# A two-layer transformer step: sums of weight chunks issued one chunk ahead, contraction halves in turn, and the norm's row spread over three chunks

## The chip, the cores and the metric

The kernel runs on one core of a Trainium2 chip. The metric is the device time of one execution in microseconds (us). The profile calls the engines PE (TensorE matmul), PEld (TensorE weight load), DVE (VectorE), ACT (ScalarE), POOL (GpSimd) and SP (SyncE, which issues most DMAs). Each engine works through its own list of instructions in the order in which the program issues them.

## What is computed

256 tokens of width 1024 pass through two layers. In each, a first feed-forward, a mixer and a second feed-forward are added to the residual; a norm ends it. All is float32.

```python
def swiglu(x, w_gate, w_up, w_down):          # 1024 -> 2816 -> 1024
    return (silu(x @ w_gate) * (x @ w_up)) @ w_down

for layer in range(2):
    x = x + 0.5 * swiglu(rms_norm(x), ...)     # feed-forward 1 (3)
    h = rms_norm(x)
    x = x + (hybrid mixer if layer == 0 else short convolution mixer)(h)
    x = x + 0.5 * swiglu(rms_norm(x), ...)     # feed-forward 2 (4)
return rms_norm(x, final_norm)
```

The hybrid mixer is a gated MLP over token chunks next to causal attention of four heads; the convolution mixer is `(b * conv3(c * xin)) @ w_out` with three projections b, c, xin.

## The kernel before

**Weights and parts.** Every float32 product is made from two parts of each operand: a high part, rounded to the matmul's format, and a low part, the remainder. `Weights` streams the weights in chunks of 1 MB. A chunk is loaded into one of five raw buffers (`load_piece`, L71, a DMA of SyncE's queue), its high part is made on ScalarE (`high`, L93) and its low part on VectorE (`low`, L98). The low part frees the raw buffer, and that lets the next load be issued. `W.next()` hands out the parts of a chunk and first calls `catch_up` (L108): high parts up to three chunks ahead (`AHEAD`), low parts up to two ahead, then whatever was queued with `afterwards` (L105).

**Sum units.** A feed-forward has 22 blocks of 128 columns: two in the opening pair of chunks (`open_pairs`), three plain units of four blocks each (`plain`, four chunks), and two sum units (`summed`, seven products each). A sum unit computes a 2 by 2 block product with seven products in place of eight; the operands are sums and differences of blocks. The sums of weights are VectorE instructions over whole chunks (`sum`, L90): one for product 1, two for product 2 and one for product 6 of the unit. In `catch_up` (L111) they are issued directly ahead of the high part of their chunk. The sums of activations are made by `Sums.make` (L490), each with a high part on ScalarE and a low part on VectorE (L503).

**The order of a feed-forward** is written out by hand: `ORDER = "nnsnsnsnssnsnsnsnsnssnsssn"`, where n is the next chunk of a plain unit and s the next product of a sum unit. Letters counted from 0 are called steps. A plain step has 24 matmuls of 512 columns, a sum step 12 (`mm_n`, L293 to L295). After each step the loop of L622 calls `run_later()`, which takes one entry of a list and may turn a finished block with four transposes into PSUM bank `misc(1)` (`turned`, L523), and then what `head` (L621) holds for that step. The turned block is read from the bank by `split`: a high part on ScalarE (L402) and a low part on VectorE (L405). The last sum unit's two turns are called those of r, the plain units' those of v.

**The norm.** The rows are scaled by the inverse root only after the first matmuls. `column` (L366) has two matmuls for the sum of squares (L369) and a chain of ten small VectorE operations (`rsqrt`, L306 to L317). `broadcast` (L373) makes two diagonal tiles on VectorE (L377), a matmul that spreads them over the partitions (L379) and a copy on ScalarE (L381). In `ffn`, `column` stands ahead of the two `added` calls (a ScalarE copy, L415, and a VectorE add, L421, which read the opening pairs from PSUM); `first`, with `broadcast`, the gating of the opening pair and `xs.gained`, follows step 0.

**After the steps.** The down projection of the first three feed-forwards takes `mm_run` (L274: two matmuls of 512 columns, two of 256, for two blocks), with a `run_later()` ahead of each half. The fourth keeps tokens on partitions (L1078 on); there `back` (L1045) first turns the residual back with 16 transposes and four VectorE copies (L1055). In the hybrid mixer two projections for the gate use `t_pair` with `mm_run`; `gate` (L901) adds the two halves of the PSUM tile and multiplies by the row. In the convolution mixer `column` stands after the first two projections and `broadcast` after the third (L1011 to L1021). In the first feed-forward, hook 20 runs `turn_small` (L716), whose transposes use `misc(1)` too.

The lines that set the order of the sums before:

```python
    def catch_up(self):
        n = min(len(self.items), self.used + AHEAD)
        while self.highs < n:
            self.sum(self.highs)
            self.high(self.highs, 0, self.tile(self.highs).shape[1])
        self.flush(min(len(self.items), self.used + AHEAD - 1))
```

## Time and profile before

| | |
|---|---|
| three runs | 1002.9, 1004.84, 1005.6 us; median 1004.84 |
| the profiled execution | 1002.79 us, of which the span of instructions is 1000.9 us |
| TensorE (PE) busy | 940.8 us, 94%, 4884 matmuls |
| weight loads (PEld) | 798.1 us, 80%, beside the matmuls |
| VectorE (DVE) busy | 729.7 us, 73% |
| ScalarE (ACT) busy | 505.0 us, 50% |
| mean granted TensorE clock | 0.981 |

A busy PE is modelled from its instructions' starts and lasts past the start of the next, so 94% is no measure of its rate; the idle time before a matmul, and what ended it, tells where TensorE stood still. In a timeline, the number in brackets is the idle time before the first instruction of the row, and behind the arrow stands what ended it.

### The profile page before, as it was taken

What the parts mean: (1) busy time and instruction counts of PE and PEld (TensorE: products, weight loads), DVE (VectorE), ACT (ScalarE), POOL (GpSimd) and SP (SyncE); (2) the same over time, 40 slices, a digit from 0 to 9 for tenths busy, and PEclk for the clock granted to TensorE, in tenths of its full rate; (3) what the DMA queues carried; (4) which work ended last, traced back from release to release, by engine and by line L of the source; (5) the groups of instructions that cost most, each with busy time, mean ns of one, the idle gap of its engine ahead of it and who ended that gap; (6) DMA issues with size and microseconds to landing.
All of it is one profiled execution on the core that took longest, in us unless ns stands there. A gap on an engine that the chain in (4) does not pass through costs nothing.

```text
span 1000.9 us, 11781 instructions
## 1 busy us (share of the span) xinstructions
PE 940.8 (94%) x4884; PEld 798.1 (80%) x4884; DVE 729.7 (73%) x742; ACT 505.0 (50%) x512; POOL 2.8 (0%) x9
## 2 busy tenths in 40 slices
PE   7989889999899989999999999999899988999897
PEld 6778778888788778778877887788899877877786
DVE  6799876566567899884758989664667768889552
ACT  6555554444645665453436556443444544656342
POOL 0000000000000000000000000000000000000000
PEclk9899999999999999999999999999999999999999
DMA  9257565647144355685424565847554515747601
GB/s 330 93 169 230 168 211 179 207 162 233 61 151 145 103 175 196 212 259 187 165 96 160 171 210 181 278 145 238 168 169 152 185 46 167 267 132 271 210 22 43
DMA packets 121169, 173.82 MB, mean 174 GB/s; under 512 B 3408, under 2 KB 69532, under 8 KB 121116
## 3 DMA queue, kind: packets, MB, share of 16 engines
q1 hardware_dynamic: 120780, 172.53, 52.3%
q8 instruction: 38, 0.62, 0.3%
q10 hardware_dynamic: 336, 0.54, 0.1%
q14 instruction: 15, 0.12, 0.0%
HBM read 172.01 MB, written 1.05 MB: 173 GB/s over the span
## 4 chain that ended last, share of the span: by engine, by line
PE 72%; DVE 16%; ACT 5%; issue 3%; DMA 3%; SPq 0%; DVEq 0%; ACTq 0%
PE ps L279 15%; PE ps L294 9%; PE ps L295 9%; PE ps L293 9%; PE ps L281 7%; DVE wlo L98 7%; PE ps L271 4%; DVE raw L90 3%; PE misc L294 3%; PE misc L295 2%; PE misc L293 2%; PE ps L287 2%; PE ps L289 2%; PE ps L288 2%; PE ps L272 2%
## 5 line engine op out<-in xcount | busy, mean ns | idle before, releaser
L93 ACT ACTIVATE whi<-raw 128x2048 fp32r<-128x2048 f32 (+2 forms) x196 | 354.7, 1824 | 216.3 <-DVE raw L90 97.7
L98 DVE TENSOR_TENSOR wlo<-raw,whi 128x2048 fp32r<-128x2048 f32 (+2 forms) x196 | 423.7, 2179 | 24.6 <-ACT whi L93 24.3
L294 PE MATMUL ps<-wlo,x 128*128 128x512 f32 x512 | 205.2, 401 | 16.1 <-DVE wlo L98 16.1
L293 PE MATMUL ps<-whi,x 128*128 128x512 f32 x512 | 207.9, 406 | 5.9 <-DVE ev_u L421 3.2
L295 PE MATMUL ps<-whi,x 128*128 128x512 f32 x512 | 204.4, 399 | 0.0
L279 PE MATMUL ps<-hx,whi 128*128 128x512 f32 x528 | 166.9, 397 | 0.0
L294 PEld LDWEIGHTS ps<-wlo,x 128*128 128x128 f32 x512 | 99.5, 194 | 40.0 <-DVE wlo L98 19.6
L293 PEld LDWEIGHTS ps<-whi,x 128*128 128x128 f32 x512 | 99.3, 194 | 26.9 <-DVE ev_u L421 3.3
L281 PEld LDWEIGHTS ps<-hx,wlo 128*128 128x128 f32 x528 | 99.0, 187 | 24.1
L295 PEld LDWEIGHTS ps<-whi,x 128*128 128x128 f32 x512 | 99.0, 193 | 21.4
L281 PE MATMUL ps<-hx,wlo 128*128 128x256 f32 x528 | 105.4, 281 | 0.0
L387 DVE SCALAR_TENSOR_TENSOR xT<-ps,xT 128x512 f32<-128x512 f32 x40 | 27.5, 691 | 74.4 <-PE ps L281 67.6
L279 PEld LDWEIGHTS ps<-hx,whi 128*128 128x128 f32 x528 | 80.8, 189 | 0.0
L90 DVE TENSOR_TENSOR raw<-raw 128x2048 f32<-128x2048 f32 x32 | 73.2, 2287 | 3.3 <-DMA raw<-in_ffn_w_up 3.0
L287 PE MATMUL ps<-x,whi 128*128 128x256 f32 x192 | 54.6, 284 | 0.0
L288 PE MATMUL ps<-x,whi 128*128 128x256 f32 x192 | 54.3, 283 | 0.0
L289 PE MATMUL ps<-x,wlo 128*128 128x256 f32 x192 | 54.3, 283 | 0.0
L271 PE MATMUL ps<-x,whi 128*128 128x512 f32 x128 | 45.2, 395 | 0.5 <-ACT whi L93 0.5
L405 DVE TENSOR_TENSOR hx<-misc,hx 128x512 fp32r<-128x512 f32 x40 | 27.5, 687 | 23.2 <-ACT hx L402 23.2
L402 ACT ACTIVATE hx<-misc 128x512 fp32r<-128x512 f32 x40 | 23.6, 589 | 27.9 <-PE misc L530 27.9
L288 PEld LDWEIGHTS ps<-x,whi 128*128 128x128 f32 x192 | 36.8, 192 | 0.0
L287 PEld LDWEIGHTS ps<-x,whi 128*128 128x128 f32 x192 | 36.8, 192 | 0.0
(247 smaller groups left out, 1179.2 us busy)
## 6 DMA issues: line engine op xcount, KB each, us to landing
raw<-in_ffn_w_gate SPq DMA_DIRECT2D x43, 1024.0 KB, 5.3
raw<-in_ffn_w_up SPq DMA_DIRECT2D x43, 1024.0 KB, 5.1
raw<-in_ffn_w_down SPq DMA_DIRECT2D x34, 1024.0 KB, 5.2
raw<-in_conv_w_in SPq DMA_DIRECT2D x12, 1024.0 KB, 5.3
raw<-in_hyb_w_in SPq DMA_DIRECT2D x10, 1024.0 KB, 6.1
raw<-in_ffn_w_down SPq DMA_DIRECT2D x12, 768.0 KB, 4.8
raw<-in_hyb_w_out SPq DMA_DIRECT2D x4, 1024.0 KB, 5.3
raw<-in_conv_w_out SPq DMA_DIRECT2D x4, 1024.0 KB, 5.1
```

The lines of the kernel that those rows point to most:

```text
L90: self.nc.vector.tensor_tensor(self.raw[dst][0], self.raw[x][0], self.raw[y][0], op=op)
L93: self.nc.scalar.activation(self.part(i, "whi")[:, s:e], self.tile(i)[:, s:e], AF.Copy)
L98: self.nc.vector.tensor_tensor(lo[:, s:e], raw[:, s:e], hi[:, s:e].bitcast(F32), op=ALU.subtract)
L271: nc.tensor.matmul(dst, whi, x, start=start, stop=False, skip_group_check=True)
L279: nc.tensor.matmul(dst, ws[i][0], xs[i], start=start and i == 0, stop=False, skip_group_check=True)
L281: nc.tensor.matmul(dst[:, :S], ws[i][1], xs[i][:, :S], start=False, stop=stop and i == n - 1, skip_group_check=True)
L287: nc.tensor.matmul(dst[:, :S], whi, x[:, :S], start=start, stop=False, skip_group_check=True)
L288: nc.tensor.matmul(dst[:, :S], whi, x[:, S:], start=False, stop=False, skip_group_check=True)
L289: nc.tensor.matmul(dst[:, :S], wlo, x[:, :S], start=False, stop=stop, skip_group_check=True)
L293: nc.tensor.matmul(dst, xhi, whi, start=start, stop=False, skip_group_check=True)
L294: nc.tensor.matmul(dst, xhi, wlo, start=False, stop=False, skip_group_check=True)
L295: nc.tensor.matmul(dst, xlo, whi, start=False, stop=stop, skip_group_check=True)
```

## The change

- The sums of a chunk are no longer issued with its high part. `sums(n)` keeps its own count, and `catch_up` calls it last, for one chunk beyond the high parts; so the sums of a chunk stand on VectorE behind the low part and the queued operations of the step before.
- A plain unit takes its chunks as gate, up, gate, up, each pair one half of the contraction; two PSUM tiles are open side by side, and silu comes after the third chunk, not the second.
- `column` now ends with the two diagonal tiles. In a feed-forward it follows step 0, `first` follows step 1, and `xs.make(0)` step 2. The two `added` calls stand ahead of it all.
- The turns of a sum unit come one step later (`turned(..., 2)`).
- In the hybrid mixer the two gate projections use `mm_s` (three matmuls of 256 columns into one half of PSUM), and `gate` is one multiply from PSUM.
- In the convolution mixer `column` follows the third projection and `broadcast` the fourth.
- `back` moves from ahead of the last down projection into it, behind the third block of weights; the PSUM tiles there are named.

```diff
-    def sum(self, i):
-        for dst, x, y, op in self.items[i].sums:
-            self.nc.vector.tensor_tensor(self.raw[dst][0], self.raw[x][0], self.raw[y][0], op=op)
+    def sums(self, n):
+        while self.summed < min(len(self.items), n):
+            for dst, x, y, op in self.items[self.summed].sums:
+                self.nc.vector.tensor_tensor(self.raw[dst][0], self.raw[x][0], self.raw[y][0], op=op)
+            self.summed += 1
...
         while self.highs < n:
-            self.sum(self.highs)
+            self.sums(self.highs + 1)
             self.high(self.highs, 0, self.tile(self.highs).shape[1])
         self.flush(min(len(self.items), self.used + AHEAD - 1))
+        self.sums(self.used + AHEAD + 1)
...
     def plain_unit(g, u, c):
-        for w in (g, u):
-            for k in range(0, KB, 4):
+        for k in range(0, KB, 4):
+            for w in (g, u):
                 yield chunk(w[:, k:k + 4, c])
...
             rsqrt(self.rstd, m[:, :NT], 1.0 / D)
+            self.diag = act.tile([P, NT, P], F32, tag="diag", bufs=1, name="diag")
+            for t in range(NT):
+                nc.vector.tensor_scalar(self.diag[:, t], ident, self.rstd[:, t:t + 1], None, op0=ALU.mult)
...
-            later.extend([None, lambda: turn(0), None, lambda: turn(1)])
+            later.extend([None] * n + [lambda: turn(0)] + [None] * (2 - n) + [lambda: turn(1)])
...
-            s = []
-            for j in range(2):
-                p = ps(1 + j)
-                for i in range(2):
+            p, s = [None, None], []
+            for i in range(2):
+                for j in range(2):
                     w = W.next()
+                    if i == 0:
+                        p[j] = ps(1 + j)
...
-                        turned(v, f)
+                            times(p[1][:, t], t, v[t], s[t])
+                        turned(v, f, 1)
...
-            turned([q16, q15], f)
+            turned([q16, q15], f, 2)
...
         ps_pairs = opened or open_pairs(norm.x)
-        norm.column()
         g0, u0 = (added(p, tag) for p, tag in zip(ps_pairs, ("ev_g", "ev_u")))
...
-        head = {0: first, 1: lambda: xs.make(0), 3: lambda: xs.make(1), 5: lambda: xs.make(2), 6: lambda: xs.make(3)}
+        head = {0: norm.column, 1: first, 2: lambda: xs.make(0), 3: lambda: xs.make(1), 5: lambda: xs.make(2),
+                6: lambda: xs.make(3)}
...
     def gate(p):
-        u = by_token(added(p, "ev_u"), norm.rbc, "ev_u")
+        u = act.tile([P, 2 * S], F32, tag="ev_u", bufs=2, name="u")
+        nc.vector.tensor_tensor(pair(u), p[:, :, :S], norm.rbc2, op=ALU.mult)
...
-    u_ps = t_pair(norm.x, scores)
+    u_ps = t_pair(norm.x, scores, mm_s)
...
-    u_ps = t_pair(norm.x, mix)
+    u_ps = t_pair(norm.x, mix, mm_s)
...
-    norm.column()
     W.catch_up()
     cp, xp = first[0], pair(first[1])
     bp = pair(copied(conv_pair(), "ev_u"))
+    norm.column()
     W.flush()
+    cn = copied(conv_pair(), "ev_g")
     norm.broadcast()
...
-            cn = copied(conv_pair(), "ev_g")
...
-            p2 = ps()
+            p2 = ps(1 + c)
...
-    back()
...
-    p0, p1 = ps(), ps()
+    p0 = ps(0)
...
             down(y0[t], w, fs[0], fs, t, 0, 512)
+        if fs[0] == 8:
+            back()
+    p1 = ps(1)
```

## Rows read from the trace of the kernel before

**Rows 1.** The page, part 1: busy time and share of the span by engine.

```profile
PE 940.8 (94%) x4884; PEld 798.1 (80%) x4884; DVE 729.7 (73%) x742; ACT 505.0 (50%) x512; POOL 2.8 (0%) x9
```

**Rows 2.** TensorE's waits: line, waited for, total us, times, longest us.

```profile
PE ps L294 <- DVE wlo L98: 16.1, 8, 3.1
```

**Rows 3.** Windows: stretch, length, busy us and instructions by engine, clock, DMA share, GB/s.

```profile
324.00:355.00 31.00, 26.04 (x109) 20.84 (x108) 25.41 (x29) 18.64 (x24) 0.00 (x0) 0.94 0.30 101
329.00:337.00 8.00, 5.53 (x19) 4.12 (x18) 5.62 (x8) 2.33 (x4) 0.00 (x0) 0.79 0.37 131
```

**Rows 4.** Timeline of VectorE, head of the second feed-forward: start us, us, instruction, idle.

```profile
324.64 0.16 DVE L306 TENSOR_SCALAR rs_v<-misc 128x2 f32<-128x2 f32 x1 [4.34 <-PE misc L369]
...
327.69 4.49 DVE L98 TENSOR_TENSOR wlo<-raw,whi 128x2048 fp32r<-128x2048 f32 x2
...
347.12 4.61 DVE L90 TENSOR_TENSOR raw<-raw 128x2048 f32<-128x2048 f32 x2
351.65 2.28 DVE L98 TENSOR_TENSOR wlo<-raw,whi 128x2048 fp32r<-128x2048 f32 x1
...
355.23 0.69 DVE L503 TENSOR_TENSOR xp<-xs,xp 128x512 fp32r<-128x512 f32 x1 [0.70 <-ACT xp L502]
```

**Rows 5.** Timeline of TensorE, head of the second feed-forward.

```profile
328.63 0.39 PE L293 MATMUL ps<-whi,x 128*128 128x512 f32 x1
...
329.77 0.39 PE L295 MATMUL ps<-whi,x 128*128 128x512 f32 x1
332.63 1.22 PE L379 MATMUL misc<-diag,ones 128*128 128x256 f32 x2 [2.47 <-DVE diag L377]
...
353.99 0.50 PE L294 MATMUL ps<-wlo,x 128*128 128x512 f32 x1 [2.49 <-DVE wlo L98]
```

**Rows 6.** The page, part 6: DMA issues, count, KB each, median us to landing.

```profile
raw<-in_ffn_w_up SPq DMA_DIRECT2D x43, 1024.0 KB, 5.1
```

**Rows 7.** Timelines of TensorE and VectorE, heads of feed-forwards 1, 3 and 4.

```profile
55.38 0.50 PE L294 MATMUL ps<-wlo,x 128*128 128x512 f32 x1 [2.91 <-DVE wlo L98]
...
517.98 0.16 DVE L306 TENSOR_SCALAR rs_v<-misc 128x2 f32<-128x2 f32 x1 [5.17 <-PE misc L369]
...
546.27 0.50 PE L294 MATMUL ps<-wlo,x 128*128 128x512 f32 x1 [1.35 <-DVE wlo L98]
...
805.96 0.16 DVE L306 TENSOR_SCALAR rs_v<-misc 128x2 f32<-128x2 f32 x1 [4.34 <-PE misc L369]
...
836.54 0.50 PE L294 MATMUL ps<-wlo,x 128*128 128x512 f32 x1 [2.91 <-DVE wlo L98]
```

**Rows 8.** Timelines of VectorE and TensorE, feed-forward 2, second sum unit and end.

```profile
398.99 0.68 DVE L405 TENSOR_TENSOR hx<-misc,hx 128x512 fp32r<-128x512 f32 x1
...
402.91 4.62 DVE L90 TENSOR_TENSOR raw<-raw 128x2048 f32<-128x2048 f32 x2 [1.03 <-DMA raw<-in_ffn_w_up]
...
409.78 0.50 PE L294 MATMUL ps<-wlo,x 128*128 128x512 f32 x1 [1.14 <-DVE wlo L98]
...
442.94 1.75 DVE L98 TENSOR_TENSOR wlo<-raw,whi 128x1536 fp32r<-128x1536 f32 x1
...
443.08 0.66 PE L530 MATMUL misc<-ident,r 128*128 128x128 f32 x4 [1.67 <-DVE hx L405]
```

**Rows 9.** Timeline of TensorE: turn_small, the convolution mixer, the fourth feed-forward's end.

```profile
130.04 0.33 PE L254 MATMUL misc<-ident,rows 128*128 128x128 f32 x1 [2.30 <-DVE hx L405]
...
719.61 0.70 PE L379 MATMUL misc<-diag,ones 128*128 128x256 f32 x2 [3.18 <-DVE diag L377]
...
926.19 0.55 PE L1052 MATMUL ps<-ident,xT 128*128 128x128 f32 x3 [1.07 <-DVE v L539]
...
934.06 0.63 PE L530 MATMUL misc<-ident,v 128*128 128x128 f32 x4 [2.65 <-DVE hx L405]
```

**Rows 10.** Windows in which mm_run and mm_s run, columns as above.

```profile
455.00:495.00 40.00, 40.00 (x230) 34.80 (x229) 20.83 (x21) 17.25 (x17) 0.00 (x0) 1.00 0.54 178
725.00:765.00 40.00, 40.00 (x335) 40.00 (x335) 28.67 (x37) 17.97 (x17) 0.00 (x0) 1.00 0.53 170
```

More of the change, by code (lines that the diff above doesn't have):

```diff
@@ L58, in __init__ @@
         self.shapes = {name: tuple(src.shape) for name, src in self.src if src is not None}
-        self.loaded = self.highs = self.lows = self.used = 0
+        self.loaded = self.summed = self.highs = self.lows = self.used = 0
         self.raw, self.parts, self.queue = {}, {}, []
@@ L371, in column @@
             rsqrt(self.rstd, m[:, :NT], 1.0 / D)
+            self.diag = act.tile([P, NT, P], F32, tag="diag", bufs=1, name="diag")
+            for t in range(NT):
+                nc.vector.tensor_scalar(self.diag[:, t], ident, self.rstd[:, t:t + 1], None, op0=ALU.mult)
         def broadcast(self):
-            diag = act.tile([P, NT, P], F32, tag="diag", bufs=1, name="diag")
-            for t in range(NT):
-                nc.vector.tensor_scalar(diag[:, t], ident, self.rstd[:, t:t + 1], None, op0=ALU.mult)
             m = misc()
-            nc.tensor.matmul(m[:, :S], ones, diag.rearrange("p t i -> p (t i)"), start=True, stop=True)
+            nc.tensor.matmul(m[:, :S], ones, self.diag.rearrange("p t i -> p (t i)"), start=True, stop=True)
             self.rbc = act.tile([P, 1, S], F32, tag="rbc", bufs=1, name="rbc")
@@ L521, in gated, with turned @@
             h[:2] = split(v, 0, True)
-        def turned(v, f):
+        def turned(v, f, n):
             def turn(q):
@@ L556, in plain @@
                             s.append(act.tile([P, 512], F32, tag="ev_g", bufs=2, name="s"))
-                            silu(s[t], p[:, t], t)
+                            silu(s[t], p[0][:, t], t)
                     if i and j == 1:
@@ L560, in plain @@
                         for t in range(NT):
-                            times(p[:, t], t, v[t], s[t])
-                        turned(v, f)
+                            times(p[1][:, t], t, v[t], s[t])
+                        turned(v, f, 1)
                     yield
```

2 lines of the change are left out of this document (1 added, 1 removed).

## The prediction, made before the change was run

> **What bounds the kernel now.** I read the page first. TensorE is busy for 94% of the span [rows 1], so the only time to win is what it loses between matmuls. The waits of TensorE come next: the largest group is the low part of a weight chunk, 16.1 us in 8 waits [rows 2]. Then I looked at the stretch in which a feed-forward begins, in the windows and the timelines of VectorE and TensorE. There VectorE, not TensorE, sets the pace: 25.41 us busy out of 31 in the second feed-forward, while TensorE has two holes [rows 3 to 5]. The reader should see two things in [rows 4, 5]. The broadcast (L379) waits 2.47 us for diag, which stands behind two low parts of 4.49 us. And the low part of step 5 runs from 351.65, directly behind two sums of 4.61 us, and TensorE stands still for 2.49 us until it is there. I count steps by the letters of ORDER, from 0. A plain step is 24 matmuls, a step of a sum unit 12. From 328.63 to 329.77 five starts took 1.14 us, 0.228 each [rows 5], so these steps take 5.5 and 2.75 us.
>
> **Working.** The profiled execution took 1002.79 us (span 1000.9), 2.05 under the median of 1004.84. The sum is made against 1002.79 and the difference then carried to the median.
>
> *The head of a feed-forward.* Four edits go together here: sums one chunk ahead, column after step 0, diag inside column, first after step 1 and make(0) after step 2. Before, the rsqrt chain of column runs ahead of the two adds that read the opening pairs; it starts at 324.64 [rows 4], having waited for the column matmuls, and the first add could have started about 0.4 earlier, at 324.2, when ScalarE's copy was done. The diag wait goes: in the new order VectorE does adds, two low parts, one sum, rsqrt and diag, about 1.3 + 4.4 + 2.2 + 2.5 = 10.4 us, so diag is there at 334.8, and TensorE wants it after steps 0 and 1, at 324.2 + 11 + 0.4 = 335.6. That hides it by 0.8 us; if that cover is gone, the wait stands again, shorter than 2.47.
>
> What is late next is xs.parts[0], which step 4 multiplies. Its make(0) now follows step 2, and step 2's catch_up puts the two sums of item 6 on VectorE ahead of it. Up to that point the new order asks VectorE for exactly the operations that the old one did before 351.65: rsqrt, two adds, diag, three low parts and the one of step 2, three sums, the gating and xs. Their work is 25.41 less 2.9 for what lies behind 351.65 in the window: 22.5 us [rows 3, 4]. I add 0.7 twice for the round trips through ScalarE (silu, xp), by the 0.70 at 355.23 [rows 4], and 0.4 for hops inside the rsqrt chain, together 24.3. So xs.parts[0] is there at 324.2 + 24.3 = 348.5. TensorE, unhindered through steps 0 to 3, comes to it at 335.9 + 2.75 + 5.5 = 344.2 and waits some 4.4 us: a new stall. Step 4 takes 2.75, step 5 begins at 351.3. Before, its second matmul came at 353.99 [rows 5], as if it had begun at 353.8. The head gains 2.5 us, not the 5 us of its two waits.
>
> Can the two sums start on time? They need a load that the low part of step 1 sets free, at about 337; loads land after 5.1 us [rows 6], at 342.1, just when VectorE is through with what stands before them. I take no wait.
>
> The same sum for the others [rows 7]: in the third, VectorE can begin at 517.98 - 0.4 = 517.6; xs.parts[0] at 541.9, step 5 at 544.7 against 546.27 - 0.2: gain 1.3. In the fourth, 805.96 - 0.4 = 805.6, plus 1.0 because TensorE itself must wait for the adds to free its bank and the broadcast comes later by that; step 5 at 833.6 against 836.3: gain 2.7. In the first, TensorE is late and throttled, VectorE waits about 3 us for the column and for the broadcast, and step 5 comes out at 55.3 against 55.2: 0, with 1.7 either way for the clock.
>
> *The second sum unit.* Before, sums stand between the low part of step 15 and that of step 16, wait 1.03 us for their load, and TensorE then loses 1.14 at step 18 [rows 8]. Ahead of their chunk the sums still need a load freed by the low part just before, plus 5.1. I get sums from 398.9 to 403.4 and the low part at 406.3, with TensorE there at 407.3: that wait goes. But the turn of r is one step later, so its half on VectorE, at 398.99 before and ahead of the sums [rows 8], falls behind them, to 404.1, and the next turn wants the same bank at 402.1: a wait of 2.0. Net, with small change elsewhere, -0.4 in feed-forwards 2 to 4. In the first the small angle operations fill the same place; 0, with the same bounds.
>
> *Step 20 of the first.* turn_small wants the bank that turn has just filled; it waits 2.30 us [rows 9]. The sum of item 24, before in step 21, now stands ahead of the freeing operation: 2.2 us more, a loss.
>
> *The end of a feed-forward.* Before, two turns of r collide and TensorE waits 1.67 us [rows 8]. Now 16 matmuls lie between them (16 times 0.174 [rows 10], 2.8 us), but the next low part (1.75 us, at 442.94 [rows 8]) comes ahead of the freeing operation too: 0.2 + 1.4 + 1.7 + 0.7 = 4.0 us after step 25, against 3.1. 0.8 to 0.9 remain; gain with the overlap 1.1 each in the first three. In the fourth, back moves away from the turns: waits of 1.07 and 2.65 go [rows 9], 1.3 comes: 2.4. Its 16 transposes and four copies are only moved, to a place where both banks are free, so 0; without that cover it costs what it saves.
>
> *Conv mixer.* The wait for diag, 3.18 [rows 9], goes: a whole pair, 48 matmuls at 0.119 [rows 10] or 5.7 us, lies between column and broadcast, against some 5 us of rsqrt, diag and a low part. Convolution starts later against TensorE, but its results are wanted two pairs later. Gain 3.2.
>
> *Hybrid mixer.* mm_s makes three matmuls of 256 columns where mm_run makes 512 + 256. By counts, 40/335 times 3 is 0.358 us, 40/230 times 2 is 0.348 [rows 10]: 32 times 0.010, a loss of 0.3. The Trainium skill, "TensorE: Matmul & The Clock Gate", section "Back-to-back issue gap", gives a warm gap of N/2.4 + 2.5 ns; an estimate by it is 2.5 ns per step more, 0.1 us instead of 0.3, so the row is taken. The gate's copy and add give way to one multiply in the same place of VectorE's queue; 0, bounds -0.7 and +0.7.
>
> *Interleaved halves* (plain): same matmuls, silu one step before times instead of two; a step of 2.75 or more covers it: 0.
>
> *Clock.* A stall can drop the clock to its lower level: 0.79 over 8 us is 1.7 us lost [rows 3]. The 31 us window has 0.94, or 1.9 us, so nearly all of its loss is this one fall, and the wait ending at 353.99 cost none before 355. The new stall at step 4 is longer than either. In feed-forwards 2 and 3 this is a new fall; VectorE, the pacer, takes up part of it: I take 0.7 of 1.7 each, -1.4.
>
> **Sum.** First: 0 + 0 - 2.2 + 1.1 = -1.1. Second: 2.5 - 0.4 + 1.1 = 3.2. Third: 1.3 - 0.4 + 1.1 = 2.0. Fourth: 2.7 - 0.4 + 2.4 = 4.7. Conv 3.2, hybrid -0.3, clock -1.4. Together 10.3: 992.5 for the profiled execution, **994.5** at the median. Bounds of the terms, 1.7 for each head and 2 for each place in the second unit, mostly independent, make 989 to 1000 the forecast's own range.
>
> **Rivals.**
> 1. *The stalls simply go.* If make(0) is not late, the four heads give up to 4.4 each more, 17.6 in all: 977. For it: the change removes every named wait of the heads. Against: 22.5 us of VectorE work must come before step 4 in any order in which the sums of item 6 precede make(0). Chance 0.10.
> 2. *The clock.* Each new stall (step 4, the turn at step 16) costs a full fall. That is 2 more us in the heads and 1.7 in each of three second units, 7 in all: 1001.5. For it: 2.47 us idle was enough for one fall. Against: 2.49 us was not. Chance 0.17.
> 3. *Slower: loads.* Sums ahead in VectorE's one queue wait for a load with every later operation behind them, at items 6 and 19, eight times. Each microsecond by which the load lands later than low part plus 5.1 costs TensorE up to one; from 1.3 us each the gain is used up, at 2.5 us (half a landing) it is 1004.8 + 8 x 1.2 = 1014. For it: one such wait of 1.03 is in the trace already. Against: the median landing is 5.1 us [rows 6], which the sum already holds. Chance 0.08.
> 4. *The sums do not move in effect.* In a busy queue only their place against evictions changes; if heads give nothing and only conv and the last tail remain, less 2.2 and 0.3, the result is about 1002 to 1004. Against: VectorE idles 5.6 of the 31 us of the head [rows 3], and the new order closes most of it. Chance 0.05.
>
> The forecast has 0.60.
>
> **How the numbers follow.** 994.5 is the likeliest case. The range 983 to 1002 takes in that case, the clock, and part of the first rival; outside stay the rest of it, the slower one and part of the fourth. A measurement of this kernel tells about 0.3%, 3 us, from no change, so faster means below 1001.8. That holds for the forecast, the first rival, and most of the second, whose full price ends just on that edge, so that any fall that is missing or partly covered leaves it below: 0.60 + 0.10 + 0.13 = 0.83. The slower side is the third rival, 0.08. The rest of the second and the fourth lie between, 0.09.
>
> **What would show it.** In the profile after: no waits of L379 for diag in feed-forwards 2 and 3 or the conv mixer; TensorE waiting 4 to 5 us at step 4 for xs.parts[0] (L503), with two sums just ahead on VectorE; none for the low part of step 5; about 2 us at the turn after step 16; about 4.5 us at turn_small. If step 4 does not wait, the head is read wrongly and the time is nearer 977; if sums wait for loads at item 6, the third rival stands.

## The result, and the profile after

Four runs of the changed kernel took 992.16, 993.75, 994.8 and 995.61 us, median **994.27**. Four of the kernel before took 1002.9 to 1006.53, median 1005.22. The ratio is 0.9892, with an interval of 0.9866 to 0.9918: faster by 1.1%, as forecast (994.5).

The profiled execution of after took 995.61 us (span 993.8) and was the longest of its four; that of before took 1002.79, less than any of its own four. The two traces therefore differ by 7.1 us of span where the medians differ by 10.95. Where the 3.8 us between these two figures come from is told below.

The page of after, part 1, answers to [rows 1]: TensorE does 32 matmuls more (the hybrid mixer's gate) and is as full as before.

```profile
PE 944.7 (95%) x4916; PEld 803.9 (81%) x4916; DVE 729.3 (73%) x740; ACT 506.4 (51%) x510; POOL 2.9 (0%) x9
```

TensorE's waits after: line, what it waited for, us in all, times, longest. In the changed kernel lines stand some three further on: mm_n is L296 to L298, the turn of a block L533, its low part L408, the low part of a chunk L100, a sum L91, the parts made by `Sums.make` L505 and L506; in the experiments the numbers can differ by one to three.

```profile
PE ps L296 <- ACT xp L505: 13.0, 4, 3.6
PE misc L533 <- DVE hx L408: 11.6, 8, 2.7
PE ps L296 <- DVE ev_g L424: 5.4, 1, 5.4
PE misc L257 <- DVE hx L408: 3.8, 1, 3.8
PE ps L290 <- ACT vg L818: 3.7, 1, 3.7
PE ps L296 <- DVE ev_u L424: 1.4, 1, 1.4
```

The group of [rows 2], 16.1 us for low parts, is gone, and so are the three waits for diag. In their place stand four waits of step 4 for `xs.parts[0]`, one in each feed-forward, 13.0 us. The turns (L533) wait eight times where they waited four: three of the four were second turns of r [rows 8] and one a turn of v [rows 9], while after it is the second turn of either sum unit, whose tile is r in both, in each feed-forward. And turn_small waits 3.8 us in place of 2.3. The two openings that have nothing ahead of them (feed-forwards 1 and 4) wait 5.4 + 1.4 = 6.8 us; before, the same places had 4.0 for the column's sums and 3.2 + 2.6 for the adds, 9.8.

The timeline of VectorE after, head of the second feed-forward, answers to [rows 4].

```profile
325.80 0.69 DVE L424 TENSOR_TENSOR ev_g<-ev_g,ps 128x512 f32<-128x512 f32 x1 [3.96 <-ACT ev_g L418]
...
331.50 2.29 DVE L91 TENSOR_TENSOR raw<-raw 128x2048 f32<-128x2048 f32 x1
...
335.67 0.48 DVE L377 TENSOR_SCALAR diag<-ident,rstd 128x128 f32<-128x128 f32 x2
...
343.58 4.62 DVE L91 TENSOR_TENSOR raw<-raw 128x2048 f32<-128x2048 f32 x2
...
349.49 0.69 DVE L506 TENSOR_TENSOR xp<-xs,xp 128x512 fp32r<-128x512 f32 x1 [0.69 <-ACT xp L505]
```

This is the order that the prediction counted: adds, two low parts, one sum, rsqrt, diag; then two sums, and behind them the first activation sum. The low part of `xs.parts[0]` ends at 350.18, which is 24.4 after the first add; the prediction had 24.3. From 326 to 350 VectorE idles little more than the 0.54 and 0.69 us in which it waits for ScalarE.

The timeline of TensorE after: turn_small, then the head, the second sum unit and the end of the second feed-forward, the convolution mixer and the last end. It answers to [rows 5, 8, 9].

```profile
130.43 0.48 PE L257 MATMUL misc<-ident,rows 128*128 128x128 f32 x1 [3.77 <-DVE hx L408]
...
337.10 0.59 PE L382 MATMUL misc<-diag,ones 128*128 128x256 f32 x2
...
345.51 0.39 PE L298 MATMUL ps<-whi,x 128*128 128x512 f32 x1
349.51 0.79 PE L296 MATMUL ps<-whi,xp 128*128 128x512 f32 x1 [3.61 <-ACT xp L505]
350.10 0.63 PE L297 MATMUL ps<-wlo,xp 128*128 128x512 f32 x1
350.53 0.63 PE L298 MATMUL ps<-whi,xp 128*128 128x512 f32 x1
...
408.00 0.66 PE L533 MATMUL misc<-ident,r 128*128 128x128 f32 x4 [2.22 <-DVE hx L408]
...
446.40 0.66 PE L533 MATMUL misc<-ident,r 128*128 128x128 f32 x4 [0.52 <-DVE hx L408]
...
717.33 0.50 PE L372 MATMUL misc<-ones,sums 128*128 128x1 f32 x4
...
723.53 0.59 PE L382 MATMUL misc<-diag,ones 128*128 128x256 f32 x2
...
924.44 0.66 PE L533 MATMUL misc<-ident,r 128*128 128x128 f32 x4 [1.07 <-DVE hx L408]
```

The broadcast at 337.10 and the one at 723.53 have no bracket: they wait for nothing. Step 4 waits 3.61. Behind that wait the matmuls start 0.43 apart (350.10 to 350.53) where 512 columns take 0.228 at the full clock [rows 5]: the clock has fallen. The turn after step 16 waits 2.22, the second turn at the end 0.52 (1.67 before), and at the last end 1.07 is left of 1.07 + 2.65.

The windows of after, columns as in [rows 3].

```profile
324.00:355.00 31.00, 27.39 (x114) 22.15 (x114) 26.89 (x31) 20.70 (x25) 0.00 (x0) 0.89 0.35 110
348.00:355.00 7.00, 5.49 (x13) 4.29 (x14) 5.61 (x7) 5.57 (x6) 0.00 (x0) 0.51 0.18 36
256.00:263.00 7.00, 5.82 (x28) 5.82 (x29) 0.00 (x0) 5.43 (x8) 0.00 (x0) 0.51 0.11 37
600.00:605.00 5.00, 5.00 (x18) 3.97 (x17) 4.90 (x4) 3.48 (x4) 0.00 (x0) 0.66 0.38 106
```

In the head, VectorE's busy time rose from 25.41 to 26.89 of 31 us; the granted clock sank from 0.94 to 0.89, and nearly all that it lost is one stretch of 7 us at 0.51, the lower of the two levels (1.2 of 2.4 GHz). The fall at 600 to 605 is new too, behind the turn of the third feed-forward; in before the same stretch has 1.00.

**Where the time came from.** The spans are cut at the same instructions of TensorE: E, the first turn of r at the end of a feed-forward, and T, the first turn of v, after step 6. Before, E stands at 152.01, 440.82, 633.03 and 924.52; after, at 153.45, 442.47, 635.69 and 919.98. T of feed-forwards 2 to 4 stands at 362.14, 554.43, 846.29 before and 363.20, 554.58, 841.39 after; step 0 of the second begins (with the column's matmuls before, without them after) at 324.10 and 325.66. The last column is a second profile of the same feed-forwards: the kernel of experiment 7, which differs from after only in the order of a few operations in the convolution mixer, and takes as long there (E at 152.69, 440.31, 631.67, 915.55; T at 361.56, 553.03, 837.07; step 0 at 323.91; span 989.4).

| stretch | predicted gain, us | after | second profile |
|---|---|---|---|
| start to E1 | -2.2 | -1.4 | -0.7 |
| E1 to step 0 of 2 (end, hybrid mixer) | 1.1 - 0.3 = 0.8 | -0.1 | 0.9 |
| step 0 of 2 to T2 (head) | 2.5 - 0.7 = 1.8 | 0.5 | 0.4 |
| T2 to E2 | -0.4 | -0.6 | -0.1 |
| E2 to T3 (end, head) | 1.1 + 1.3 - 0.7 = 1.7 | 1.5 | 0.9 |
| T3 to E3 | -0.4 | -2.5 | 0.0 |
| E3 to T4 (end, conv mixer, head) | 1.1 + 3.2 + 2.7 = 7.0 | 7.6 | 7.9 |
| T4 to E4 | -0.4 | -0.4 | -0.3 |
| E4 to the end | 2.4 | 2.6 | 2.5 |
| sum | 10.3 | 7.1 | 11.5 |

**The clock's share.** For every run the span and the mean granted clock are known. Span times (1 - clock) is the shortfall: the microseconds that the clock's falls would cost if TensorE had worked through all of them. For after's four runs it is 23.9, 21.8, 19.8 and 23.8, for spans of 993.8, 992.0, 990.4 and 993.0: the run with the least shortfall is the shortest. Before's profiled run has 1000.9 x 0.019 = 19.0, and the 16 runs of before that stood beside the first experiments have a median of 22.1. So the median of after (22.8) loses 0.7 more than that of before, while the two profiled runs differ by 4.9. That is 4.2 us, about the 3.8 that were to be explained. Between the medians, 0.7 of shortfall leaves 10.95 + 0.7, some 11.7, for everything else; the prediction's sum without its clock term was 10.3 + 1.4 = 11.7. That the two agree to the tenth is luck: the clock is given to a thousandth, which is 1 us of span.

### The profile page after: what moved, and what is told of

The parts are those of the page before. It is cut to its first block, busy times and chain, and to the rows that moved or that the text cites. A ratio compares the mean times of both kernels' runs of the same rounds, so it can differ in the third digit from the quotient of the medians.

```text
span 993.8 us, 11866 instructions
## 1 busy us (share of the span) xinstructions
PE 944.7 (95%) x4916; PEld 803.9 (81%) x4916; DVE 729.3 (73%) x740; ACT 506.4 (51%) x510; POOL 2.9 (0%) x9
## 4 chain that ended last, share of the span: by engine, by line
PE 68%; DVE 20%; DMA 6%; ACT 3%; issue 3%; SPq 0%; DVEq 0%
PE ps L282 13%; PE ps L296 9%; PE ps L298 9%; PE ps L297 9%; DVE wlo L100 8%; PE ps L284 7%; DVE raw L91 6%; DMA raw<-in_ffn_w_up 5%; PE ps L274 4%; PE ps L290 3%; PE ps L291 3%; PE ps L292 3%; PE ps L275 2%; PE misc L296 2%; PE misc L297 2%
## 5 line engine op out<-in xcount | busy, mean ns | idle before, releaser
L100 DVE TENSOR_TENSOR wlo<-raw,whi 128x2048 fp32r<-128x2048 f32 (+2 forms) x196 | 423.3, 2177 | 21.3 <-ACT whi L95 21.1
L296 PE MATMUL ps<-whi,x 128*128 128x512 f32 x512 | 204.7, 400 | 6.8 <-DVE ev_g L424 5.4
L297 PE MATMUL ps<-wlo,x 128*128 128x512 f32 x512 | 201.4, 393 | 0.1
L298 PE MATMUL ps<-whi,x 128*128 128x512 f32 x512 | 201.4, 393 | 0.0
L296 PEld LDWEIGHTS ps<-whi,x 128*128 128x128 f32 x512 | 97.5, 190 | 27.7 <-DVE ev_g L424 5.7
L298 PEld LDWEIGHTS ps<-whi,x 128*128 128x128 f32 x512 | 97.1, 190 | 21.1
L297 PEld LDWEIGHTS ps<-wlo,x 128*128 128x128 f32 x512 | 97.5, 190 | 20.5 <-DVE wlo L100 0.5
L91 DVE TENSOR_TENSOR raw<-raw 128x2048 f32<-128x2048 f32 x32 | 73.2, 2288 | 12.2 <-DMA raw<-in_ffn_w_up 12.0
L390 DVE SCALAR_TENSOR_TENSOR xT<-ps,xT 128x512 f32<-128x512 f32 x40 | 27.4, 690 | 70.2 <-PE ps L284 62.6
L290 PE MATMUL ps<-x,whi 128*128 128x256 f32 x224 | 65.1, 291 | 3.7 <-ACT vg L818 3.7
L291 PE MATMUL ps<-x,whi 128*128 128x256 f32 x224 | 64.4, 288 | 0.0
L292 PE MATMUL ps<-x,wlo 128*128 128x256 f32 x224 | 64.4, 288 | 0.0
L290 PEld LDWEIGHTS ps<-x,whi 128*128 128x128 f32 x224 | 44.0, 197 | 4.0 <-ACT vg L818 4.0
L408 DVE TENSOR_TENSOR hx<-misc,hx 128x512 fp32r<-128x512 f32 x40 | 27.4, 686 | 26.7 <-ACT hx L405 26.7
L291 PEld LDWEIGHTS ps<-x,whi 128*128 128x128 f32 x224 | 44.1, 197 | 0.0
L292 PEld LDWEIGHTS ps<-x,wlo 128*128 128x128 f32 x224 | 44.1, 197 | 0.0
```

Of the source, the lines that this page charges most:

```text
L91: self.nc.vector.tensor_tensor(self.raw[dst][0], self.raw[x][0], self.raw[y][0], op=op)
L100: self.nc.vector.tensor_tensor(lo[:, s:e], raw[:, s:e], hi[:, s:e].bitcast(F32), op=ALU.subtract)
L290: nc.tensor.matmul(dst[:, :S], whi, x[:, :S], start=start, stop=False, skip_group_check=True)
L291: nc.tensor.matmul(dst[:, :S], whi, x[:, S:], start=False, stop=False, skip_group_check=True)
L292: nc.tensor.matmul(dst[:, :S], wlo, x[:, :S], start=False, stop=stop, skip_group_check=True)
L296: nc.tensor.matmul(dst, xhi, whi, start=start, stop=False, skip_group_check=True)
```

## The experiments

After the result the theory was that of the prediction: VectorE's work ahead of step 4 sets the head of a feed-forward, and the order of the operations only chooses which part comes late. Its rivals: the order is worth something by itself, by a way not yet seen; or one small part (diag made earlier, back moved) carries the gain. Each ratio below is to the kernel before on the same chip. The median of after, 994.27, is the other mark. The last two columns are medians over a kernel's runs, each of its own, so that they do not add up exactly; within one kernel the last one spreads by 2 to 7 us, and differences of 1 or 2 us in it tell nothing. In the expectations e3, e5 and e6 are experiments 8, 9 and 10.

| kernel | median us | ratio (interval) | shortfall | time less shortfall |
|---|---|---|---|---|
| before | 1004.7 | 1 | 22.1 | 983.6 |
| after | 994.27 | 0.9892 (0.9866 to 0.9918) | 22.8 | 971.8 |
| 1 sums back | 998.63 | 0.9928 (0.9904 to 0.9952) | 25.9 | 974.3 |
| 2 head back | 1002.08 | 0.9962 (0.9938 to 0.9986) | 23.0 | 978.8 |
| 3 low parts first | 1024.51 | 1.0186 (1.0153 to 1.0219) | 25.6 | 998.7 |
| 4 sums alone | 1016.4 | 1.0107 (1.0089 to 1.0125) | 27.4 | 989.1 |
| 5 diag alone | 1000.81 | 0.995 (0.9936 to 0.9965) | 21.0 | 979.6 |
| 6 back alone | 999.85 | one run | 19.0 | 980.9 |
| 7 conv back | 992.4 | 0.9862 (0.9818 to 0.9905) | 22.3 | 971.2 |
| 8 turn early | 989.22 | 0.9827 (0.9785 to 0.9868) | 19.7 | 968.5 |
| 9 small late | 983.9 | 0.9779 (0.9741 to 0.9818) | 18.7 | 965.3 |
| 10 sum in the opening | 976.51 | 0.9701 (0.9669 to 0.9734) | 14.6 | 961.2 |
| 11 angles late | 975.97 | 0.9711 (0.9693 to 0.973) | 12.7 | 963.3 |

**1. The sums go back to their own step**, all else as after.

```diff
         self.flush(min(len(self.items), self.used + AHEAD - 1))
-        self.sums(self.used + AHEAD + 1)
```

> The changed kernel with one line taken out: sums are issued again directly ahead of their chunk's high part, and with that ahead of the low part of the same step; everything else as changed. Theory A (in a feed-forward's head VectorE's total work sets the time; the order of the sums only chooses who waits): the 3.3 to 4 us waits for xp at step 4 go, and the wait for the low part of step 5 comes back at about the same size, so the heads stay within 1 us each; in the second unit the turn at step 16 no longer waits (2.6 us in feed-forward 2) and the low part of step 18 waits again for 1 to 1.5 us; turn_small waits 2.3 in place of 3.8 us. Together 2 to 6 us faster than the changed kernel: 988 to 992. Theory B (the sums one chunk ahead are what made the change faster): 999 to 1004.

It took 4.4 us more than after, just under the range of theory B, so theory A missed: the order is worth something by itself. Its waits of TensorE, and the timelines of ScalarE and VectorE in the second head:

```profile
PE ps L296 <- DVE wlo L100: 18.1, 8, 3.9
PE ps L295 <- ACT xp L504: 7.2, 4, 2.1
```

```profile
337.65 1.92 ACT L95 ACTIVATE whi<-raw 128x2048 fp32r<-128x2048 f32 x1 [6.36 <-DVE raw L91]
339.47 0.37 ACT L383 ACTIVATE rbc<-misc 128x256 f32<-128x256 f32 x1
...
349.20 0.69 DVE L505 TENSOR_TENSOR xp<-xs,xp 128x512 fp32r<-128x512 f32 x1 [2.11 <-ACT xp L504]
```

ScalarE stands still for 6.36 us, because the next instruction of its list is the high part of a chunk whose sum VectorE has not made yet. Behind it in the list stand the copy of the row (L383), silu, xg, one more high part and the high part xp. The row itself pays little of the 6.36 us: its matmul ends at 338.91 and the copy begins at 339.47. But from 337.65 on ScalarE has hardly a pause until xp is made, and VectorE, which has two sums less to do ahead of xp than in after, waits for ScalarE for 0.65, 1.09 and 2.11 us in place of 0.54 and 0.69. So VectorE in turn waits for ScalarE, and not only for its own work: the sum of VectorE's durations is a lower bound of the head, and this order lies above it. The wait of step 4 shrinks from 13.0 to 7.2 in all, but the low parts wait again, 18.1. In the page, the idle time of ScalarE ahead of its high parts that is put down to a sum is a mark of this, before and after:

```profile
L93 ACT ACTIVATE whi<-raw 128x2048 fp32r<-128x2048 f32 (+2 forms) x196 | 354.7, 1824 | 216.3 <-DVE raw L90 97.7
...
L95 ACT ACTIVATE whi<-raw 128x2048 fp32r<-128x2048 f32 (+2 forms) x196 | 354.9, 1823 | 183.4 <-DVE raw L91 49.7
```

It is 126.7 us in this experiment and 180.2 in experiment 3. It is a mark and no measure: in experiment 4 it is 75.9, less than before, and the kernel is slower.

**2. The head goes back**: column ahead of the adds, first after step 0, make(0) after step 1; diag stays in column and the sums stay ahead.

```diff
+        norm.column()
         g0, u0 = (added(p, tag) for p, tag in zip(ps_pairs, ("ev_g", "ev_u")))
...
-        head = {0: norm.column, 1: first, 2: lambda: xs.make(0), 3: lambda: xs.make(1), 5: lambda: xs.make(2),
+        head = {0: first, 1: lambda: xs.make(0), 3: lambda: xs.make(1), 5: lambda: xs.make(2),
```

> The changed kernel with column again ahead of the two adds, first after step 0 and make(0) after step 1; the diagonal tiles stay inside column, the sums stay one chunk ahead. Theory A (VectorE's total work in the head sets the time): no wait for diag, no wait for xp at step 4, but a wait of 4 to 5 us for the low part of step 5, behind the two sums; each head within 1 us of the changed one, the fourth up to 2 us worse because the bank of the opening pair is read after the root: 994 to 999. Theory C (the spreading of the root over three chunks is what made the change faster): 1000 to 1004.

7.8 us above after: what the rival expected, and more than the theory allowed. The waits, from a profile that was the longest of its ten runs (1005.98):

```profile
PE ps L297 <- DVE wlo L100: 11.6, 6, 3.7
PE misc L372 <- DVE sums L367: 4.2, 1, 4.2
...
PE ps L296 <- DVE ev_u L424: 3.7, 1, 3.7
...
PE ps L296 <- DVE ev_g L424: 3.2, 1, 3.2
```

Step 4 hardly waits any more (0.9 in the second feed-forward), but low parts do, 11.6 in all: inside the heads one wait takes the other's place at about its size, as the theory had it. What is lost stands elsewhere: the two bare openings cost 4.2 + 3.7 + 3.2 = 11.1 us in place of 6.8: with the column ahead, TensorE must wait for the sum of squares first and then for the adds. Spreading the root over the steps takes that wait under the matmuls of step 0. The theory's expectation had this loss only in the fourth feed-forward.

**3. Low parts ahead of the sums of the same step**, meant to serve TensorE first.

```diff
+        self.flush(min(self.highs, n - 1))
         while self.highs < n:
...
-        self.sums(self.used + AHEAD + 1)
```

> The changed kernel with sums at their own chunk's step, not one ahead, but in that step behind the low part and the queued operations (one line more in catch_up: the low parts that can be made are made first). Theory A (who stands behind the sums is who waits): neither xp at step 4 nor the low part of step 5, nor the turn at step 16, nor the low part of step 18 stands behind the two sums; what stands behind them is the high part of their own chunk, three steps ahead of its use. The waits of 3.3 to 4 us at step 4 shrink below 1, a wait of up to 2.6 us for the low part of step 6 is new, the second unit has none, turn_small waits 2.3 us. 10 to 18 us faster than the changed kernel: 976 to 984. Rival (VectorE's total work alone sets the time of a feed-forward): the same waits come at steps 6 to 8 in full size, 990 to 994.

Both theories were wrong by 30 us and more: it is slower than before. ScalarE's timeline shows the mechanism of the first experiment at a larger size:

```profile
342.98 1.92 ACT L95 ACTIVATE whi<-raw 128x2048 fp32r<-128x2048 f32 x1 [8.56 <-DVE raw L91]
...
362.05 1.92 ACT L95 ACTIVATE whi<-raw 128x2048 fp32r<-128x2048 f32 x1 [7.55 <-DVE raw L91]
```

A sum that goes 2.29 us later on VectorE holds up all that stands behind its high part on ScalarE, whose results VectorE and TensorE want next. Here the row pays too: its matmul ends at 342.04, and ScalarE copies it at 344.80. TensorE waits 15.7 us for xp (13.0 in after), 14.9 and 0.8 for low parts and 6.0 and 1.0 for high parts (none in after); at turns and at turn_small it waits less than in after.

**4. The sums one chunk ahead, alone**, put into the kernel before.

```diff
-            self.sum(self.highs)
+            self.sums(self.highs + 1)
...
+        self.sums(self.used + AHEAD + 1)
```

> The kernel before, with one part of the change: the sums one chunk ahead, behind the low parts. Theory (who stands behind the sums is who waits; high parts that wait for sums stop ScalarE's queue): in the heads the sum of item 4 now stands ahead of diag and lengthens its wait from 2.5 to 4.7 us, and the wait for the low part of step 5 shrinks by as much; in the second unit, where the turn of r is not late, the waits at step 18 (1.1 to 1.3 us, 3.1 in the first with its fall of the clock) go; turn_small waits 1.5 longer: 4 to 7 us faster than before, 998 to 1001. Rival (sums ahead only block the evictions behind them): no gain, 1003 to 1007.

Both sides missed: this part alone makes the kernel 1.1% slower. The wait for diag grew to 4.67 us in the second head, as the theory had it; what failed is that the wait for the low part of step 5 hardly shrank, to 1.95 from 2.49, and those at step 18 stayed. The timeline of VectorE in the second head, and the waits of TensorE:

```profile
337.84 2.29 DVE L91 TENSOR_TENSOR raw<-raw 128x2048 f32<-128x2048 f32 x1
340.04 0.48 DVE L380 TENSOR_SCALAR diag<-ident,rstd 128x128 f32<-128x128 f32 x2
```

```profile
PE ps L297 <- DVE wlo L100: 15.8, 8, 4.1
PE misc L382 <- DVE diag L380: 12.5, 3, 4.7
...
PE misc L257 <- DVE hx L408: 4.5, 1, 4.5
```

With diag still in broadcast, the sum now stands ahead of diag: those waits grow from 8.1 to 12.5, turn_small's from 2.3 to 4.5, together 6.6 us, and the low parts' stays (15.8 for 16.1). VectorE waits for ScalarE's xp as in experiment 1: 2.78 us in the second head, 1.76 in before. Less the shortfall, the kernel is 5.9 above before on the same chip; the shortfall itself grew by 5.3. So the first edit of the change pays only in company: in after it is worth 4.4 us (experiment 1), in before it costs 11. That the third edit, diag in column, is the company that it needs is argued from the waits for diag; the two alone were not run.

**5. The diag tiles in column, alone**, in the kernel before.

```diff
             rsqrt(self.rstd, m[:, :NT], 1.0 / D)
+            self.diag = act.tile([P, NT, P], F32, tag="diag", bufs=1, name="diag")
+            for t in range(NT):
+                nc.vector.tensor_scalar(self.diag[:, t], ident, self.rstd[:, t:t + 1], None, op0=ALU.mult)
```

> The kernel before, with one part of the change: the two diagonal tiles made in column, right behind the root. Theory A (VectorE's work sets the heads): the three waits for diag, 8.1 us, all go, but in feed-forwards 2 and 3 only VectorE's own idle time while it waited for the row (1.7 and 1.2 us) is gained and the wait for the low part of step 5 grows by the rest; the convolution mixer's 3.2 us are gained whole: 5 to 7 us faster than before, 998 to 1000. Rival (a wait that goes is gained): 8.1 us and two falls of the clock, 3.4: 993 to 994.

The gain is 4.6 us, just short of what the theory expected and far from the rival's. The 8.1 us of waits for diag go, but in its waits

```profile
PE ps L294 <- DVE wlo L98: 19.7, 8, 3.7
```

the low parts take 3.6 back (16.1 before): in a feed-forward's head the wait moves on, in the convolution mixer it goes for good. The waits in the two bare openings grow by 1.7 in all, where the diagonal tiles now stand ahead of the adds; the theory had not counted these.

**6. back moved into the last down projection, alone**, in the kernel before.

```diff
         for t in range(NT):
             run_later()
             down(y0[t], w, fs[0], fs, t, 0, 512)
+        if fs[0] == 8:
+            back()
```

> The kernel before, with one part of the change: back moved behind the third block of the last down projection. Theory: the waits of 1.07 and 2.65 us around back go, the collision of the two turns of r, 1.7 us, comes in their place: from the start of the first turn of r to the end of the span 2.0 to 2.5 us less than the 76.4 of before; the time as a whole within the noise of one run, 1000 to 1004.

From the first turn of r (923.86) to the end of the span (998.0) it took 74.1 us where before took 1000.9 - 924.52 = 76.4: 2.2 gained, as expected. The time as a whole, of one run, came out just under the range, and tells nothing by itself. The turns at that place:

```profile
923.86 0.60 PE L530 MATMUL misc<-ident,r 128*128 128x128 f32 x4
926.12 0.66 PE L530 MATMUL misc<-ident,r 128*128 128x128 f32 x4 [1.66 <-DVE hx L405]
```

The waits of 1.07 and 2.65 [rows 9] are gone, and the collision of two turns, 1.66, has come in their place, as in the other three [rows 8].

**7. The conv mixer goes back**: column and broadcast at the places that they had before, diag still in column.

```diff
+    norm.column()
     W.catch_up()
...
-    norm.column()
     W.flush()
-    cn = copied(conv_pair(), "ev_g")
     norm.broadcast()
```

> The changed kernel with the convolution mixer's column and broadcast at their old places; the diagonal tiles stay inside column. If the 3.2 us of the convolution mixer come from the diagonal tiles alone, which now stand ahead of the low parts: no wait for diag, 994 to 995. If they come from the move of column and broadcast: the wait of 3.2 us is back, 997 to 998.

Nearest to the diag tiles alone, though below both ranges: no slower than after: 992.4, and less the shortfall 971.2 for 971.8. From the column's matmuls to the broadcast it takes 707.55 to 713.75, 6.20 us, as after (717.33 to 723.53), with no wait in it. The diag tiles alone are the 3.2 us of the conv mixer (experiment 5 has no wait there either); the move that the prediction credited is not needed for it. The kernel is also the second profile of the table above.

**8. The turns of the first sum unit one step earlier again**; those of the second stay.

```diff
-            turned([q16, q15], f, 2)
+            turned([q16, q15], f, 1 if f < 10 else 2)
```

> The changed kernel, where the first sum unit's two turns are not delayed (the second unit's still are). Theory A (the wait of 1.7 to 2.7 us at the turn after step 16 comes from the VectorE half of the turn before, which stands behind the two sums): that wait goes in all four feed-forwards; in its place the low part of step 18, behind the same sums, makes TensorE wait about 1 us. 4 to 8 us faster than the changed kernel: 986 to 990. Rival (the turn waits for VectorE's general lateness, not for the order): the wait only moves to step 18 in full size, 993 to 995.

As expected, 5 us below after. Its waits:

```profile
PE ps L297 <- DVE wlo L100: 4.7, 3, 4.1
...
PE misc L533 <- DVE hx L408: 2.6, 4, 1.1
```

The turns wait 2.6 in place of 11.6; in the first feed-forward, where the angles fill the place, a low part waits 4.1 instead. Half of the gain is waits, half the clock: the shortfall is 19.7 for 22.8.

**9. turn_small one step later** as well, away from the turn that fills its bank.

```diff
-    def start_hybrid():
-        sines()
+    def turn_tables():
+        tables()
...
-    ffn(norm, nxt, {8: load_small, 15: angles, 20: start_hybrid, 21: tables}, [p for _, p in opened])
+    ffn(norm, nxt, {8: load_small, 15: angles, 20: sines, 21: turn_tables}, [p for _, p in opened])
```

> The kernel of e3_turn_early, in which turn_small of the first feed-forward also follows step 21 in place of step 20 (the sines stay after step 20). Theory (turn_small's wait of 3.8 us is for the bank that the turn just ahead of it has filled, behind the sum of item 24): the wait goes whole, with the fall of the clock behind it, 4 to 6 us faster than e3: 983 to 985. Rival (the wait is for VectorE's lateness): the wait stays at half or more, 987 to 989.

As expected: the wait of L257 is gone (L725 behind it waits 0.9 for 0.4), and 5.3 us with it.

**10. The first sum of a feed-forward in its opening**, where VectorE idles, and a low part ahead of the gating. The two edits were not tried apart.

```diff
         W.flush(W.used + 1)
+        W.sums(W.used + AHEAD + 2)
...
         def first():
+            W.flush()
```

> The kernel of e5_small_late, with the sum of item 4 issued still earlier, in the opening pair, where VectorE idles about 4 us ahead of the two adds (feed-forwards 2 to 4), and the low part of item 4 issued ahead of the gating, where VectorE waits for the row. Theory (VectorE's work between the adds and xs.parts[0] sets the head, 22.5 us of it): 2.2 us of that work leave, the wait for xp at step 4 falls from about 3.6 to 1.5 us in these three heads and the clock falls less often: 6 to 10 us faster than e5, 974 to 978. Rival (the wait moves on, to the low parts of steps 5 and 6): 0 to 2 us faster, 981 to 984.

In the expected range: 976.51 us, 17.8 below after. The waits of step 4 and VectorE at the opening of the second feed-forward:

```profile
PE ps L296 <- ACT xp L506: 7.8, 4, 2.1
```

```profile
315.61 2.29 DVE L91 TENSOR_TENSOR raw<-raw 128x2048 f32<-128x2048 f32 x1
319.53 0.69 DVE L424 TENSOR_TENSOR ev_g<-ev_g,ps 128x512 f32<-128x512 f32 x1 [1.63 <-ACT ev_g L418]
```

The sum lies in what was an idle time of 3.96 us ahead of the first add, of which 1.63 is left. Here the theory of the prediction holds in the main: 2.2 us less of VectorE's work ahead of step 4 take 1.3 us on the average from the four waits, in the second feed-forward 1.5 (2.12 for 3.61) where the expectation had 2.1; part of the rest VectorE loses in new waits for ScalarE (0.34, 0.70 and 0.69 us for 0.54 and 0.69). From after to here the waits at the turns, at turn_small and at step 4 shrank; the time less the shortfall became 10.6 us shorter and the shortfall 8.2 less.

**11. The angle operations three steps later** as well, to clear the low part's wait in the first feed-forward.

```diff
-    ffn(norm, nxt, {8: load_small, 15: angles, 20: sines, 21: turn_tables}, [p for _, p in opened])
+    ffn(norm, nxt, {8: load_small, 18: angles, 22: sines, 23: turn_tables}, [p for _, p in opened])
```

> The kernel of e6_sum_in_opening, in which the small angle operations of the first feed-forward follow step 18 in place of 15, and the sines and turn_small steps 22 and 23. Theory (the wait of 3.9 us for the low part of step 18 in the first feed-forward is the angles' 3.1 us on VectorE behind the two sums): it goes, 3 to 5 us with the clock: 971 to 973.5. Rival (VectorE is late there anyway): the wait moves to steps 20 to 22, 975 to 977.

No gain that can be told (975.97), as the rival had it. The wait of 3.8 us for the low part of step 18 went to 0.7, smaller ones came, 2.6 in all for 4.3, and the transposes of turn_small, after step 23, now wait behind VectorE's gains, 3.3 us for 0.9:

```profile
PE misc L727 <- DVE gains_mix L259: 3.3, 1, 3.3
```

## Why the prediction was right, and where it was not

**The heads: right in mechanism.** The waits for diag and for the low part of step 5 went, and step 4 waits for `xs.parts[0]`, late behind two sums, at the time that the count gave (24.3 against 24.4 after the first add). The broadcast came 0.95 after diag was made (0.8 predicted). The wait is 3.61 in the second feed-forward against 4.4 predicted, because the first matmul needs only the high part, which is there 0.7 ahead of the low one. What was mis-sized in feed-forwards 2 and 3 is the clock of the new stall. The step said "I take 0.7 of 1.7 each"; in the second, the fall lasts 7 us at 0.51 (3.4 us short, against 1.7 in the fall before) and in the second profile 7 us at 0.54, and the head gives 0.5 and 0.4 for 1.8. In the third it is the whole 1.7 (0.76 over 541 to 548, in the second profile 0.76 over 540 to 547). The second rival, a full fall at each new stall, was right of these two heads; of the turns after step 16 in feed-forwards 2 to 4 it was not: the fall of the third came in one profile and not in the other.

**The first feed-forward: mis-sized.** The head was put at 0; T stands at 64.18 after and 65.17 before, a gain of 1.0, since the bare opening lost less with the column behind step 0 (experiment 2). The loss at turn_small came, but smaller: 3.77 for 2.30 is 1.5 more, where 2.2 was forecast. The clock over 129 to 137 was 0.79 before, 0.57 in after and 0.79 in the second profile, and the start to E1 loses 1.4 and 0.7 for 2.2.

**The second sum unit: right.** The wait for the low part of step 18 went, the turn after step 16 waits 2.22 for a predicted 2.0 (in part luck, see the loads below). In the second profile the stretch loses 0.1, 0.0 and 0.3 for 0.4 each; after's 2.5 in the third is a wait of like size with a fall behind it (600 to 605, clock 0.66).

**The ends and back: right.** 0.52 is left of 1.67 (0.8 to 0.9 predicted); the last end gives 2.5 to 2.6 for 2.4, and 2.2 of it by the move of back alone.

**The conv mixer: right in size, wrong in reason.** The wait went, 3.2 us. But not because "a whole pair, 48 matmuls" lies between column and broadcast: it lies there in the old places too (6.20 us from one to the other in experiment 7, as in after), and with diag in column the wait goes there as well.

**The hybrid mixer: right.** E1 to step 0 gives 0.9 in the second profile for 1.1 - 0.3; in after a stretch at the lower clock, 256 to 263, stands in it. The matmuls themselves show the price: three of the four groups of eight steps ran at the full clock in both traces, and each took 2.87 us before (the third from 278.93 to 281.79) and 2.95 after (280.33 to 283.29), 0.010 per step. That is 0.3 for 32 steps, the row's price. The estimate of 0.1 by the Trainium skill, "TensorE: Matmul & The Clock Gate", section "Back-to-back issue gap", does not agree with these traces.

**Loads: the third rival's mechanism is there, without its price.** VectorE's sums waited 12.0 us for loads, in nine waits, where they had waited 3.0. Eight of the nine, 0.9 to 1.8 us each, are in the second sum units; at item 6, where the prediction looked for the sign of this rival, there is one, of 0.25. In the page after:

```profile
L91 DVE TENSOR_TENSOR raw<-raw 128x2048 f32<-128x2048 f32 x32 | 73.2, 2288 | 12.2 <-DMA raw<-in_ffn_w_up 12.0
```

One of them is the sum at the second unit of the second feed-forward, which begins 2.2 later than worked out (402.73, where 398.9 + 1.6 for the later begin of this feed-forward was due):

```profile
398.63 2.28 DVE L100 TENSOR_TENSOR wlo<-raw,whi 128x2048 fp32r<-128x2048 f32 x1
402.73 4.62 DVE L91 TENSOR_TENSOR raw<-raw 128x2048 f32<-128x2048 f32 x2 [1.81 <-DMA raw<-in_ffn_w_up]
```

TensorE came to its turn later than worked out by about as much, so this shows only in that turn's 2.22, and the match with the predicted 2.0 is of two terms that were both about 2 us too early.

**The sum.** That 994.5 lies 0.3 us from the median is in part luck. Single stretches miss by up to 1.5 us in the second profile and by more in after, and the misses cancel. Slips in the working move little: 324.2 + 10.4 is 334.6, not 334.8, the third head's terms give 1.4, not 1.3, and the fourth rival's own terms give 1001.7.

**What the prediction did not see** is why the parts work together. It counted a head by VectorE's work and short round trips through ScalarE. Experiments 1 and 3 show the second engine in the loop: ScalarE works its list in order, and a high part that waits for a sum holds up what stands behind it. VectorE's waits for ScalarE's xp tell how much comes back to it: 15.5 us in all in before, 11.2 in after, and 17.6, 15.7, 26.5 and 19.5 in experiments 1 to 4. The count of 24.3 came out because in the new order VectorE waits for ScalarE for only 1.23 us of it, where 1.4 was allowed. In experiments 1, 3 and 4 the theories that counted without this expected times 7 to 40 us too low.

**What stays open.** Which of its falls the clock takes in a run is not explained: single profiles differ by several us in it. The worth of the parts does not add up (4.6 for diag, 11 lost by the sums, 2.2 for back, against 10.95 together), and pairs of parts were not tried. The contraction halves in turn, which the prediction put at 0, and the hybrid mixer's one multiply were in no experiment by themselves.

## What to carry to other kernels

When two engines feed each other through lists worked in order, adding up the work of the busier one gives only a lower bound: look up which instruction of the other stands ahead of the one that is wanted, and what it waits for. An operation that another engine waits for at the head of its list belongs in the idle place before the rush (here the opening, 1.8 us of TensorE's waits and of clock per feed-forward), and an edit that moves one ahead may cost time until its new place is cleared too. Compare two profiles of the same work, and each run's granted clock, before a difference of a few us in one stretch is given a cause.

## What the runs showed of the hardware that was not expected

The clock does not fall alike behind like waits. A wait of 3.74 us in the hybrid mixer (its products for vg), the same in before and after, was followed in before by a clock of 0.76 over 256 to 263, in after by 0.51, and in the second profile by 0.76 again. In before, 2.47 us of waiting brought a fall [rows 3, 5], and 3.18 in the conv mixer [rows 9] none; in experiment 4 the same 3.18 brought one (0.83 over 730 to 740). The windows of before:

```profile
256.00:263.00 7.00, 6.11 (x31) 5.50 (x32) 0.50 (x1) 5.14 (x8) 0.00 (x0) 0.76 0.07 25
...
716.00:724.00 8.00, 4.82 (x39) 4.57 (x38) 5.42 (x6) 2.78 (x3) 0.00 (x0) 1.00 1.05 340
```

Runs of one kernel spread by this: experiment 7 had spans of 986.7 at a clock of 0.987 and 994.1 at 0.976. And a kernel with shorter waits won back clock as well: from after to experiment 10 the shortfall sank from 22.8 to 14.6, 8.2 us beside 10.6 in the rest of the time.
